# The last feed-forward net: chunk 3 by seven block products too, the half-wide chunk 5 by eight

## The chip, the cores and the metric

One core of one Trainium2 chip runs the whole program. The metric is the device time of one execution in microseconds, the median of the runs. The engines are named as the profile names them: PE (TensorE), DVE (VectorE), ACT (ScalarE), POOL (GpSimd) and SP (SyncE), which issues most DMAs.

## The reference

Two layers, each with a gated feed-forward net, a mixer (short convolution, a gated recurrence, pooled windows), cross attention against a memory of 256 rows, and a second feed-forward net; a layer norm stands behind each. There are 256 tokens of width 1024, all in float32. What matters here is the net:

```python
def swiglu(x, w_gate, w_up, w_down):
    return (jax.nn.silu(x @ w_gate) * (x @ w_up)) @ w_down
...
    h = layer_norm(ALPHA * h + 0.5 * swiglu(h, ffn2_gate[l], ffn2_up[l], ffn2_down[l]),
                   ln_g[l, 3], ln_b[l, 3])
```

`w_gate` and `w_up` are 1024 x 2816, `w_down` is 2816 x 1024. The change touches only the last of the four nets (`ffn2` of the second layer); its output is the kernel's output.

## The kernel before

**Products in three parts.** Each float32 operand is split into a rounded high part (ACT, a cast, L75) and the rest (DVE, a subtraction, L76). A product is then three matmuls: high by high, high by low, low by high (`mm_rows`). Weights come from HBM in pieces of 128 x 1024 floats (512 KB) into tiles called `raw` (six buffers); the two parts of a piece go to `whi` and `wlo` (eight buffers each), which come free when PE has used them.

**Chunks.** The hidden width 2816 is cut into five chunks of 512 and one of 256 (chunk 5). For each chunk a net computes gate and up products, the gated activation in the tile `sg`, turns it by four DMAs (`dealt`, L525) and a transpose on DVE (L531, into the buffer with the tag "up"), splits it into `ah` and `al`, and later multiplies it with the rows of `w_down` in slabs of 256 rows: `both(c, u)` is slab u of chunk c, 24 matmuls of 512 columns, which add to four PSUM banks `ys` (`dn` in the profile). Tokens come in two tiles of 128.

**Three ways to do a chunk.**
- `hidden` (by eight): gate, then up, each 2 token tiles x 8 k tiles x 3 matmuls of 512 columns, 96 in all.
- `by_seven`: with tokens and k halved, the four blocks of gate and up (first and second k half: `w00` gate first, `w10` gate second, `w01` up first, `w11` up second) need seven products of blocks rather than eight, each 4 k tiles x 3 matmuls. For this the weight blocks are added in place: `parts_of(r, plus)` adds one block to another on DVE (L702) and splits the sum, and `more` adds the second k half's block onto `w01` and then onto `w00` by accumulating DMAs from POOL's queue (L738). The sums of the token blocks (`bx`, in `kTh` and `kTl`) are made once per net. Two products stay in the tile `ef` (tag "up", one buffer) until the end of the chunk. Between the block products it runs two slabs of earlier chunks (`between`). For chunk 5 the matmuls have 256 columns.
- `last_hidden` (half-wide, in columns): four calls of `mm_cols`, each 8 matmuls of 512 columns and 8 of 256. Its result comes out turned already, so that no `dealt` DMAs are needed. Until now only the first net uses it.

**Homes of the blocks.** In `by_seven` the list `homes` says in which tiles the blocks `w00`, `w01`, `w11` and `w10` lie: pairs of one-buffer tiles ("spare0", "spare1"), ("lng", "lnb"), two `raw` buffers, and for `w10` "spare2" and one `raw`.

**Which chunk goes which way.** `sevens` is (2, 4) in the first net and (2, 4, 5) in the others. `later` says how many slabs run behind a chunk that is not by seven. Because chunk 5 by seven follows chunk 4 by seven, its turn is put off, and the last down products (`ending`) begin with token tile 0 over both column halves.

**The turned memory.** `mT` holds the transposed attention memory in two tiles with the tags "mT0" and "mT1", 2048 floats per partition each. Its last reader is the value product of the last attention.

**What sets the order.** The program is traced as written above; a planner then orders each engine's queue by its own estimate of when operands and buffers are ready, earlier traced work first, and each engine works its queue strictly in that order. `issue_after` puts an instruction behind another on its engine.

Of the kernel before, what the change touches and what calls it, by code (L numbers as in the profile page):

```python
# [8 lines left out]
F32 = mybir.dt.float32  # L9
# [8 lines left out]
P = 128  # L18
DEPTH = 2
SEQ = 256  # L20
DM = 1024
# [39 lines left out]
def model(ctx: ExitStack, tc: tile.TileContext, t: dict, out: bass.AP):  # L61
    nc = tc.nc
    cst = ctx.enter_context(tc.tile_pool(name="cst", bufs=1))
# [126 lines left out]
    mT = Halves()  # L190
# [285 lines left out]
    def ffn(l, name, n, pend=None, last=False, early=None, started=None, following=None):  # L476
        gate, up, down = (t[f"{name}_{x}"][l] for x in ("gate", "up", "down"))
        with tc.tile_pool(name="ffn", bufs=2, reuse_waits="tile") as fp:
            acts = []
# [10 lines left out]
            def all_products(w):  # L490
                o = [acc((P, CHUNK)) for _ in range(NT)]
                for a in range(0, NK, 2):
                    for i in range(NT):
                        for k in range(a, a + 2):
                            products(o[i], w, i, k)
                return o

            def activations():
                return fp.tile([P, NT, CHUNK], F32, tag="sg", name="sg", bufs=1)
# [9 lines left out]
            def activate(s, i, og):  # L509
                return nc.scalar.activation(ordered(s[:, i, :]), in_order(og), AF.Silu)  # L510

            def gated(s, i, ou):
                v = ordered(s[:, i, :])
                nc.vector.tensor_tensor(v, in_order(ou), v, op=ALU.mult)
# [120 lines left out]
            def hidden(c0, between=lambda: None):  # L635
                s = activations()
                o = all_products(load(gate, 0, NK, c0, CHUNK))
                for i in range(NT):
                    activate(s, i, o[i])
                between()  # L640
                o = all_products(load(up, 0, NK, c0, CHUNK))
                for i in range(NT):
                    gated(s, i, o[i])
                return turn(s)
# [17 lines left out]
                    split(*parts[n], q[o])  # L662
                return parts

            def by_seven(c0, ncol, bx, between):
                deep = 1024 // ncol

                def rows_by_columns(r):
                    return r.rearrange("p (k c) -> p k c", c=ncol)

                def pieces(*tags):
                    return [
                        rows_by_columns(
                            (fp if "spare" in g else wp).tile([P, DM], F32, tag=g, name="raw", bufs=6 if g == "raw" else 1)
                        )
                        for g in tags
                    ]

                def part_of(m, j, i):
                    k = 4 * j + deep * i  # L680
                    return m[k * P : (k + deep) * P, c0 : c0 + ncol].rearrange("(k p) c -> p k c", p=P)

                def block(m, j, to):
                    for i, x in enumerate(to):
                        loads.append(nc.sync.dma_start(x, part_of(m, j, i)))
                    return to

                if ncol == CHUNK:
                    homes = [("spare0", "spare1"), ("lng", "lnb"), ("raw", "raw")]
                    n = sevens.index(c0 // CHUNK)  # L690
                    homes = [homes[(n + i) % 3] for i in range(3)] + [("spare2", "raw")]
                else:
                    homes = [("spare2",), ("raw",), ("raw",), ("raw",)]
                w00 = block(gate, 0, pieces(*homes[0]))
                w01 = block(up, 0, pieces(*homes[1]))
                w10 = block(gate, 1, pieces(*homes[3]))

                def parts_of(r, plus=None):
                    hi, lo = [], []
# [15 lines left out]
                def run(o, x, w, more=False):  # L715
                    for k in range(4):
                        wh, wl = w.at(k, slice(0, ncol))
                        mm_rows(o, x[0][:, k, :], x[1][:, k, :], wh, wl, k == 0 and not more, k == 3, more)
# [27 lines left out]
                run(o, part_of_x(0, 1), parts_of(w10), True)  # L746
                between[0]()
                activate(s, 0, o)
                w11 = block(up, 1, pieces(*homes[2]))
                run(total, bx[1], parts_of(w00, w11), True)  # L750
                if ncol == CHUNK:
                    more(w00, gate, 1)
# [29 lines left out]
            def last_hidden(c0, turn=None):  # L782

                ah, al = act_tiles()
                s = activations()[:, 0, :].rearrange("p (j c) -> p j c", j=2)
                r = fp.tile([P, NT, CHUNK], F32, tag="up", name="up", bufs=1)[:, 0, :].rearrange("p (j c) -> p j c", j=2)
                for m, o in ((gate, s), (up, r)):
                    if turn and m is gate:
                        with tc.issue_after(passed[-1][1].ins):
                            turn(0, 0)  # L790
                    w = load(m, 0, NK, c0, 2 * P)
                    if turn and m is gate:
                        with tc.issue_after(lows[-1].ins):
                            turn(0, 2)
                    for j in range(2):
                        add(o[:, j, :], mm_cols(w, slice(j * P, (j + 1) * P), xT))
                    if m is gate:
                        nc.scalar.activation(s, s, AF.Silu)
                nc.vector.tensor_tensor(s, r, s, op=ALU.mult)
                for j in range(2):  # L800
                    split(
                        *(x[:, j, :].rearrange("p (i b r) -> p i b r", i=2, b=4) for x in (ah, al)),
                        s[:, j, :].rearrange("p (i r b) -> p i b r", i=2, b=4),
                    )
                if turn:
                    with tc.issue_after(lows[-1].ins):
                        turn(1, 0)
                        turn(1, 2)
                return ah, al
# [4 lines left out]
                return w, ah[:, 2 * u : 2 * u + 2, :], al[:, 2 * u : 2 * u + 2, :]  # L814


            sevens = (2, 4) if early is not None else (2, 4, 5)
            passed, dealts, turn_memory = [], [], None
            bx = []

# [6 lines left out]
            chunks = [(c, min(CHUNK, DFF - c)) for c in range(0, DFF, CHUNK)]  # L827
# [13 lines left out]
                            rows_of(a, i, k, m, c == u == k == 0, apart)  # L841

            todo = [(c, u) for c in range(4) for u in range(2)]
            later = (0, 0, 0, 2, 0, 2) if early is None else (0, 1, 0, 1, 0, 2)
            for c, (c0, ncol) in enumerate(chunks):
                if not c:
                    acts.append(first()())
                    ys = [[acc((P, 512), "dn") for _ in range(2)] for _ in range(NT)]
                elif c in sevens:
                    half = []  # L850

                    def deal_last():
                        acts[4] = acts[4]()

                    left = by_seven(
                        c0, ncol, bx,
                        [lambda: both(*todo.pop(0))] * 2 if ncol == CHUNK else
                        [lambda: (half.append(slab(3, 0)), both(3, 0, half[0], (0,))), deal_last, lambda: both(3, 0, half[0], (1,))],
                    )
                else:  # L860
                    acts.append(hidden(c0)() if ncol == CHUNK else last_hidden(c0, turn_memory))
                if c == 1 and early is None:
                    bx.extend(blocks_of_x())
                if c == 5:
                    gb = ln_params(l, n)
                if c == 1 and early is not None:

                    with tc.issue_after(loads[-1].ins):
                        rest = early(fp)
                if c == 3 and early is not None:  # L870
                    with tc.issue_after(lows[-1].ins):
                        rest[0]()
                    nc.gpsimd.tensor_copy(early_memory[:, 0:2048:256], acts[2][0][:, 0, 0:8].bitcast(F32))
                    turn_memory = load_memory(fp, loads[-1])
                if c in sevens:
                    if ncol < CHUNK:
                        held = []
                        with tc.issue_after(lows[-1].ins):
                            acts[4] = acts[4](held)
                    acts.append(left() if c + 1 in sevens else left()() if c == 5 else left()()())  # L880
                    if ncol < CHUNK:
                        with tc.issue_after(passed[-1][0].ins), tc.issue_after(passed[-1][1].ins):
                            held[0]()
                        both(3, 1)
                else:
                    for _ in range(later[c]):
                        both(*todo.pop(0))
# [569 lines left out]
```

## Time and profile before

| | |
|---|---|
| runs | median 1063.42 us (1062.63 to 1063.47, 3 runs) |
| profiled execution | 1062.76 us; span 1061.1 us; granted clock 0.998 |
| PE busy | 99% of the span, 6014 matmuls |
| DVE, ACT, POOL busy | 87%, 62%, 9% |
| DMA | 251.06 MB, mean 237 GB/s |
| last net | about 887 to 1061 us |

Times in rows of the profile are microseconds from the start of the span. A row of a timeline has start, duration, engine, line and operation, the tiles written and read, a count where equal instructions were merged, and in brackets the time that the engine stood idle before it and what ended that. In a table of stretches each engine has its busy time and, in brackets, its instructions; then come the granted clock of PE, the busy share of the 16 DMA engines and GB/s.

### The profile page before, as it was taken

The page shows a single profiled execution, that of the slowest core. Times are in us where ns is not written, and L with a number is a line of the kernel's source. Part 1 is how long each engine was busy: PE and PEld are TensorE (multiplying, and loading weights), DVE is VectorE, ACT ScalarE, POOL GpSimd, SP SyncE. Part 2 cuts the span into 40 slices and gives each one's busy share as a digit, 9 for nine tenths or more (in the row PEclk, how much of TensorE's full clock was granted, in tenths as well). Part 3 has the DMA queues.
Part 4 walks back from the last instruction along what each step waited for, and adds up shares of the span by engine and source line. Part 5 has one row for each costly group of instructions (what it writes and reads, how often), then busy time and mean ns, then how long its engine had stood idle before and what let it go on. Part 6 is the DMA issues. An engine that isn't in the chain of part 4 may idle for free.

```text
span 1061.1 us, 16463 instructions
## 1 busy us (share of the span) xinstructions
PE 1051.1 (99%) x6014; PEld 934.2 (88%) x6014; DVE 922.6 (87%) x1224; ACT 662.1 (62%) x909; POOL 94.6 (9%) x128
## 2 busy tenths in 40 slices
PE   9999999999999999999999999999999999999997
PEld 7888888889899888888888888998998998888896
DVE  6998898989988789887898887999899788898787
ACT  6675775676557567655665656666774655675661
POOL 8002001000000001010001001010000000000001
PEclk9999999999999999999999999999999999999999
DMA  9999984754675589988689978876636675799961
GB/s 363 296 301 298 260 274 156 256 167 156 211 273 178 167 281 232 349 200 224 237 302 257 335 226 210 268 233 223 207 117 219 241 240 167 241 295 301 242 194 68
DMA packets 142305, 251.06 MB, mean 237 GB/s; under 512 B 11248, under 2 KB 51984, under 8 KB 142224
## 3 DMA queue, kind: packets, MB, share of 16 engines
q1 hardware_dynamic: 130656, 228.89, 64.9%
q0 software_dynamic: 10992, 19.94, 11.0%
q10 hardware_dynamic: 576, 1.18, 0.3%
q8 instruction: 47, 0.77, 0.3%
q14 instruction: 34, 0.28, 0.1%
HBM read 234.50 MB, written 1.05 MB: 222 GB/s over the span
## 4 chain that ended last, share of the span: by engine, by line
PE 99%; DMA 1%; DVE 0%; issue 0%; ACTq 0%; DVEq 0%
PE acc L132 65%; PE dn L132 31%; PE acc L199 1%; DMA h<-in_x_dram 1%; PE dn L1135 0%; PE dn L1209 0%; PE dn L1208 0%; PE dn L1197 0%; PE acc L1277 0%; PE dn L1160 0%; DVE h L412 0%; PE acc L581 0%; PE acc L338 0%; DVE h L407 0%; DVE st L383 0%
## 5 line engine op out<-in xcount | busy, mean ns | idle before, releaser
L76 DVE TENSOR_TENSOR wlo<-raw,whi 128x1024 fp32r<-128x1024 f32 (+1 forms) x452 | 533.1, 1209 | 60.7 <-ACT whi L75 54.5
L75 ACT CAST whi<-raw 128x1024 fp32r<-128x1024 f32 (+1 forms) x452 | 456.2, 1043 | 196.5 <-PE dn L132 58.3
L132 PE MATMUL acc<-whi,xT 128*128 128x512 f32 (+1 forms) x1064 | 313.8, 372 | 0.0
L132 PEld LDWEIGHTS acc<-whi,xT 128*128 128x128 f32 x1064 | 199.1, 189 | 27.2 <-DVE halves L721 0.4
L132 PE MATMUL acc<-wlo,xT 128*128 128x512 f32 (+1 forms) x532 | 197.9, 372 | 0.0
L132 PE MATMUL dn<-whi,ah 128*128 128x512 f32 x346 | 131.5, 380 | 0.0
L132 PE MATMUL dn<-wlo,ah 128*128 128x512 f32 x346 | 131.2, 379 | 0.0
L132 PE MATMUL dn<-whi,al 128*128 128x512 f32 x346 | 131.1, 379 | 0.0
L132 PE MATMUL acc<-xT,whi 128*128 128x512 f32 x480 | 117.6, 381 | 0.0
L132 PEld LDWEIGHTS acc<-wlo,xT 128*128 128x128 f32 x532 | 100.6, 189 | 13.2
L132 PEld LDWEIGHTS acc<-xT,whi 128*128 128x128 f32 x480 | 86.8, 190 | 9.8
L132 PE MATMUL dn<-whi,xT 128*128 128x512 f32 x288 | 87.8, 381 | 0.0
L132 PEld LDWEIGHTS dn<-whi,al 128*128 128x128 f32 x346 | 65.4, 189 | 9.2
L132 PEld LDWEIGHTS dn<-wlo,ah 128*128 128x128 f32 x346 | 65.4, 189 | 8.9
L132 PEld LDWEIGHTS dn<-whi,ah 128*128 128x128 f32 x346 | 65.4, 189 | 8.9
L132 PEld LDWEIGHTS acc<-xT,wlo 128*128 128x128 f32 x480 | 62.9, 191 | 3.2
L132 PE MATMUL acc<-xT,wlo 128*128 128x256 f32 x480 | 63.3, 275 | 0.0
L132 PE MATMUL acc<-whi,kTh 128*128 128x512 f32 (+1 forms) x176 | 62.0, 352 | 0.0
L132 PE MATMUL acc<-wlo,kTh 128*128 128x512 f32 (+1 forms) x176 | 61.7, 351 | 0.0
L132 PE MATMUL acc<-whi,kTl 128*128 128x512 f32 (+1 forms) x176 | 61.7, 351 | 0.0
L132 PEld LDWEIGHTS dn<-whi,xT 128*128 128x128 f32 x288 | 54.4, 189 | 7.7 <-DVE xT L76 0.2
L132 PE MATMUL dn<-wlo,xT 128*128 128x512 f32 x144 | 54.6, 379 | 0.0
(250 smaller groups left out, 1279.9 us busy)
## 6 DMA issues: line engine op xcount, KB each, us to landing
raw<-in_ffn_up_dram SPq DMA_DIRECT2D x88, 512.0 KB, 6.0
raw<-in_ffn_down_dram SPq DMA_DIRECT2D x88, 512.0 KB, 6.0
raw<-in_ffn_gate_dram SPq DMA_DIRECT2D x84, 512.0 KB, 5.8
raw<-in_w_in_dram SPq DMA_DIRECT2D x48, 512.0 KB, 4.7
dealt<-sg SPq DMA_DIRECT2D x80, 128.0 KB, 4.9
raw<-in_ffn_up_dram POOLq DMA_DIRECT2D x19, 512.0 KB, 6.2
raw<-in_ffn_gate_dram POOLq DMA_DIRECT2D x16, 512.0 KB, 9.9
raw<-in_ca_k_dram SPq DMA_DIRECT2D x16, 512.0 KB, 5.4
```

Of the source, the lines that this page charges most:

```text
L75: rounded = nc.scalar.copy(hi, src)
L76: lows.append(nc.vector.tensor_tensor(lo, src, hi.bitcast(F32), op=ALU.subtract))
L132: turns.append(nc.tensor.matmul(o, w, x, start=start, stop=stop, skip_group_check=more))
L199: turns.append(nc.tensor.transpose(pt[:, k, :], src[:, (4 * j + k) * P : (4 * j + k + 1) * P], unit))
```

## The change

In the last net `sevens` becomes (2, 3, 4): chunk 3 is computed by seven block products, and chunk 5 goes through `last_hidden`. `later` becomes (0, 0, 0, 0, 0, 2): the two slabs that ran behind chunk 3 run inside it, and the two slabs of chunk 3 run behind chunk 5. The part of `by_seven` that lays out and loads the first two blocks becomes a function of its own, `blocks_of_weights`. For chunk 3 of the last net it is called right behind chunk 0 (`begun`), with `w00` and `w01` in the two tiles of the turned memory; `w11` lies in ("lng", "lnb"). Chunk 4 has `w00` in the spares, `w01` in two `raw` buffers and `w11` in "mT0". The other nets are as before.

```diff
-            def by_seven(c0, ncol, bx, between):
+            def blocks_of_weights(c0, ncol):
                 deep = 1024 // ncol
...
                 def pieces(*tags):
+                    if "mT" in tags[0]:
+                        x = cst.tile([P, 2 * DM], F32, tag=tags[0], name="raw")
+                        return [rows_by_columns(x[:, n * DM : (n + 1) * DM]) for n in range(2)]
                     return [
...
                     homes = [homes[(n + i) % 3] for i in range(3)] + [("spare2", "raw")]
+                    if last:
+                        homes[0:3] = (
+                            (("spare0", "spare1"), ("lng", "lnb"), ("raw", "raw")),
+                            (("mT0",), ("mT1",), ("lng", "lnb")),
+                            (("spare0", "spare1"), ("raw", "raw"), ("mT0",)),
+                        )[n]
                 else:
                     homes = [("spare2",), ("raw",), ("raw",), ("raw",)]
-                w00 = block(gate, 0, pieces(*homes[0]))
-                w01 = block(up, 0, pieces(*homes[1]))
-                w10 = block(gate, 1, pieces(*homes[3]))
+                w00, w01 = (block(m, 0, pieces(*x)) for m, x in zip((gate, up), homes))
+
+                def others(m, n):
+                    return block(m, 1, pieces(*homes[n]))
+
+                return w00, w01, others, part_of
+
+            def by_seven(c0, ncol, bx, between):
+                deep = 1024 // ncol
+                w00, w01, others, part_of = begun.get(c0) or blocks_of_weights(c0, ncol)
+                w10 = others(gate, 3)
...
-                w11 = block(up, 1, pieces(*homes[2]))
+                w11 = others(up, 2)
...
-            sevens = (2, 4) if early is not None else (2, 4, 5)
+            sevens = (2, 4) if early is not None else (2, 3, 4) if last else (2, 4, 5)
+            begun = {}
...
-            later = (0, 0, 0, 2, 0, 2) if early is None else (0, 1, 0, 1, 0, 2)
+            later = (0, 1, 0, 1, 0, 2) if early is not None else (0, 0, 0, 0, 0, 2) if last else (0, 0, 0, 2, 0, 2)
...
+                if c == 0 and last:
+                    begun[chunks[3][0]] = blocks_of_weights(*chunks[3])
...
-                    acts.append(left() if c + 1 in sevens else left()() if c == 5 else left()()())
+                    acts.append(left() if c == 4 and 5 in sevens else left()() if c == 5 else left()()())
```

More of the change, by code (lines that the diff above doesn't have):

```diff
@@ L691, in by_seven, with rows_by_columns @@
                     homes = [homes[(n + i) % 3] for i in range(3)] + [("spare2", "raw")]
+                    if last:
[4 more added lines that the diff above has]
+                        )[n]
                 else:
                     homes = [("spare2",), ("raw",), ("raw",), ("raw",)]
-                w00 = block(gate, 0, pieces(*homes[0]))
-                w01 = block(up, 0, pieces(*homes[1]))
-                w10 = block(gate, 1, pieces(*homes[3]))
+                w00, w01 = (block(m, 0, pieces(*x)) for m, x in zip((gate, up), homes))
[6 more added lines that the diff above has]
+                w10 = others(gate, 3)
+                def rows_by_columns(r):
+                    return r.rearrange("p (k c) -> p k c", c=ncol)
                 def parts_of(r, plus=None):
```

## The prediction

> **What bounds the kernel now.** I read the page's engine line first, then the chain that ended last, then the table by stretches of the last net, then the timelines of PE, DVE, ACT, POOL and SP around it. The page:
>
> ```profile
> span 1061.1 us, 16463 instructions
> PE 1051.1 (99%) x6014; PEld 934.2 (88%) x6014; DVE 922.6 (87%) x1224; ACT 662.1 (62%) x909; POOL 94.6 (9%) x128
> q1 hardware_dynamic: 130656, 228.89, 64.9%
> q0 software_dynamic: 10992, 19.94, 11.0%
> PE 99%; DMA 1%; DVE 0%; issue 0%; ACTq 0%; DVEq 0%
> ```
>
> The reader is to see that TensorE alone carries the time, and VectorE is second with 87%. The chain in order of time, at the end of the last net, gives the prices of a matmul where nothing waits:
>
> ```profile
> 1031.13 1.34 PE acc L132 x12
> 1032.47 16.84 PE dn L132 x78
> 1049.31 4.03 PE acc L132 x36
> 1053.36 0.43 DVE h L371
> 1057.11 0.40 DVE h L412
> ```
>
> 78 matmuls of 512 columns in 16.84 us are 0.216 us each; 12 of 256 columns in 1.34 us and 36 in 4.03 us are 0.112 us each. Inside the last net (887 to 1053 us) PE issues at these spacings throughout; the view of waits has no row for PE there. So work taken off PE comes off the time, and any new wait on PE is added to it. The four stretches below, cut where PE begins each chunk, are chunk 2 (by seven), chunk 3 (by eight), chunk 4 (by seven), and chunk 5 (by seven, half-wide) with what follows it; columns are busy time and instructions of PE, weight load, DVE, ACT, POOL, then granted clock, DMA share, GB/s.
>
> ```profile
> 929.50:958.00 28.50, 28.50 (x133) 24.90 (x133) 26.01 (x26) 20.31 (x24) 2.37 (x2) 1.00 1.04 314
> 958.00:989.10 31.10, 31.10 (x145) 27.23 (x145) 26.21 (x26) 15.74 (x18) 2.37 (x2) 1.00 0.94 272
> 989.10:1017.60 28.50, 28.50 (x133) 24.95 (x132) 22.63 (x21) 19.13 (x22) 3.69 (x3) 1.00 0.79 211
> 1017.60:1037.00 19.40, 19.40 (x131) 17.96 (x130) 17.45 (x19) 13.74 (x18) 1.44 (x2) 1.00 0.77 231
> ```
>
> PE fills every stretch at clock 1.00; DVE and the DMA engines are near full in 929 to 989, and that is where the change puts more on both.
>
> **PE work removed and added.** Chunk 3 goes from eight block products to seven: 8 x 12 = 96 matmuls of 512 columns become 84, so 12 x 0.216 = 2.6 us go. The 48 matmuls of its two down slabs stay. Chunk 5 goes the other way. By seven it was 84 matmuls of 256 columns, 84 x 0.112 = 9.4 us. In columns by eight it is four calls of `mm_cols` with 8 matmuls of 512 and 8 of 256 columns each. That form stands in the timeline of the query product (PE rows):
>
> ```profile
> 826.00 1.89 PE L132 MATMUL acc<-xT,whi 128*128 128x512 f32 x8
> 827.73 1.05 PE L132 MATMUL acc<-xT,wlo 128*128 128x256 f32 x8
> 828.62 1.89 PE L132 MATMUL acc<-xT,whi 128*128 128x512 f32 x8
> ```
>
> From 826.00 to 828.62 is one call, 2.62 us; four are 10.5 us, 1.1 us more than before. PE work falls by 2.6 - 1.1 = 1.5 us. The order of the last down products changes (token tile 0 is no longer run early over both halves), but not their number, and the last 36 matmuls and the 7.8 us from 1053.34 us to the end of the span (norm of the second tile, store) stay; I cost that at nothing, since the rows at 1053.36 and after hang on the last matmul, not on DVE's backlog. The DVE and ACT work that chunk 5 loses (three of seven pieces, three adds, a turn through four DMAs) lies beside PE; it is worth nothing in time.
>
> **The early loads.** Chunk 3's gate and up blocks of the first k half (four DMAs of 512 KB on SP) go into the two tiles of the turned memory, traced behind chunk 0. The memory's last reader is the value product of the attention before; its last row on PE, the SP timeline from there, and the DMA share behind it:
>
> ```profile
> 862.75 0.38 PE L132 MATMUL acc<-whi,mT 128*128 128x512 f32 x1
> ```
>
> ```profile
> 864.13 6.96 SPq L103 DMA_DIRECT2D raw<-in_ffn_up_dram  x4
> 871.19 0.41 SPq L685 DMA_DIRECT2D raw<-in_ffn_gate_dram  x1
> 885.71 0.37 SPq L103 DMA_DIRECT2D raw<-in_ffn_gate_dram  x1
> ```
>
> ```profile
> 872.00:880.00 8.00, 8.00 (x39) 7.01 (x38) 2.25 (x7) 0.60 (x2) 0.00 (x0) 1.00 0.48 178
> 880.00:887.00 7.00, 7.00 (x38) 6.20 (x37) 5.94 (x10) 4.65 (x7) 0.63 (x1) 1.00 0.09 9
> ```
>
> SP issues nothing between 871.6 and 885.7 because the six raw buffers are full, and the DMA engines stand at 0.48 and 0.09. By the page the hardware queue needs 0.649 x 1061.1 / 228.89 = 3.0 us of all engines per MB, so the 2 MB take 6 us out of some 10 free ones. Cost nothing. If they came later, chunk 1's loads would be pushed back by up to those 6 us; that is the bound above.
>
> **DMA in chunks 3 and 4.** A chunk by seven loads four 1 MB blocks plainly, adds two more with accumulating transfers issued from POOL, and reads two 1 MB down slabs. The software queue (mostly these) takes 0.110 x 1061.1 / 19.94 = 5.9 us per MB. Chunk 3 so gains 2 x 5.9 = 11.7 us of DMA and has 6 us moved ahead; chunk 5 drops 0.5 MB of accumulation, 2.9 us. The stretches 958 to 1017.6 held 0.94 x 31.1 + 0.79 x 28.5 = 52 us; they get 52 + 11.7 - 6 - 2.9 = 55 us in 57. Full, but not over.
>
> The transfer with the least room is the second accumulation of a chunk: piece split (DVE), POOL issues, landing, cast (ACT), split (DVE), PE. In chunk 2 the POOL timeline has it, each row with the landing that the trace gives for that line:
>
> ```profile
> 935.23 1.18 POOL L738 DMA_DIRECT2D raw<-in_ffn_gate_dram  x1 [8.06 <-DVE wlo L76]
> 938.75 1.19 POOL L738 DMA_DIRECT2D raw<-in_ffn_gate_dram  x1 [2.34 <-DVE wlo L76]
> ```
>
> ```profile
> DMA to landing us min/median/max: 10.2/10.2/10.2
> ```
>
> Landing is 10.2 us behind the second issue. PE uses the result in the last 12 matmuls of chunk 2, from 958.0 - 2.6 = 955.4 us, 6.5 us after that landing. In chunk 4 both landed within 10.6 us of their issues at 994.1 and 995.2:
>
> ```profile
> L738 POOL DMA_DIRECT2D raw<-in_ffn_gate_dram x2: 1180/1226/1272, 994.1 to 995.2; - x2
> ...
> DMA to landing us min/median/max: 6.0/8.3/10.6
> ```
>  By the sum below, chunk 3's second accumulation goes out at about 971; it lands at 981, cast and split end at 983.5, and PE wants that second piece at 985.3. Room of 1.8 us: no stall, though a thin margin.
>
> **VectorE, the term that decides.** Rows of DVE at the seam of chunks 2 and 3:
>
> ```profile
> 950.05 4.63 DVE L76 TENSOR_TENSOR wlo<-raw,whi 128x1024 fp32r<-128x1024 f32 x4 [1.33 <-ACT whi L75]
> 954.60 0.68 DVE L721 TENSOR_TENSOR halves<-halves,acc 128x512 f32<-128x512 f32 x1
> 955.19 2.35 DVE L76 TENSOR_TENSOR wlo<-raw,whi 128x1024 fp32r<-128x1024 f32 x2
> 960.33 1.22 DVE L775 TENSOR_TENSOR sg<-sg,halves 128x1024 f32<-128x1024 f32 x1
> 968.55 1.30 DVE L531 STREAM_TRANSPOSE square<-dealt 128x512 f32<-128x512 f32 x2 [0.18 <-DVE wlo L76]
> 971.60 1.23 DVE L76 TENSOR_TENSOR al<-square,ah 128x1024 fp32r<-128x1024 f32 x1 [0.63 <-ACT ah L75]
> ```
>
> One operation of 1024 columns costs DVE 1.14 us in a row of them (the fourth starts 3.41 us behind the first, at 1.22 us each). A chunk by seven has 18 splits (seven blocks and two slabs of two pieces), 4 adds (L702, the same shape), the gate product and the split behind the turn: 24 x 1.14 = 27.4 us, and 2 x 0.6 for L721 and 1.2 for L531: 29.8 us, against 28.5 us of PE (132 x 0.216). Chunk 3 by eight needs 12 splits, one turn and little else, some 17 us against 31. So today chunk 3 is where DVE catches up; after the change three chunks follow each other that each cost DVE 1.3 us more than PE, and only its lead carries it: at most eight pieces, the depth of `whi` and `wlo`.
>
> The lead at the seam: of the four splits from 950.05, two end chunk 2 (952.4) and two are chunk 3's first block (954.7). Then two L721 and the second block (two adds, two splits) end at 954.7 + 1.2 + 4.6 = 960.5; PE, starting chunk 3 at 958.0, wants that last piece three half-runs later, at 961.9. Lead 1.4 us. One chunk later DVE has 29.8 us behind it and PE 28.5, and the gate product of chunk 3 (1.14 us) now falls ahead of the same piece: 1.4 - 1.3 - 1.1 = -1.0. So a stall of 1.0 us in chunk 4, or none if the planner lets the gate product wait, which it can (its reader is a chunk away). Less than none is excluded, since PE has no wait to lose. The end above is a DVE that also waits: in 929.5 to 958 it was idle 28.5 - 26.0 = 2.5 us. If each of chunks 3 and 4 kept that, 1.0 + 5.0 = 6.0 us. I take 0.5, between the two placements, since the wait at 950.05 was for a cast that itself had waited for a landing, which a late DVE meets less.
>
> **What ACT waits for.** The copy out of chunk 3's second product goes into the one "up" buffer, which is free only when chunk 2's turned block is split (today 971.60 plus 1.2, 15 us into chunk 3). It stands in ACT's queue with casts behind it. The silu of chunk 3 likewise waits for the one `sg` buffer until chunk 2's four deal DMAs have landed (about 968.5). PSUM is not short: four banks, three in use at that time. If the planner knows these times, casts go ahead of the copy; today's nearest case is the silu at chunk 1, which held ACT:
>
> ```profile
> 918.59 0.60 ACT L510 ACTIVATE sg<-acc 128x512 f32<-128x512 f32 x1 [4.20 <-DMA dealt<-sg]
> ```
>
> ACT stood 4.2 us there and PE lost nothing, with eight pieces of lead. I cost it at nothing; the end above is again those 4.2 us, where DVE's lead is gone.
>
> **The sum.** -2.6 + 1.1 + 0.5 = -1.0 us. The profiled execution took 1062.76 us (span 1061.1 and 1.7 around it) and lies 0.66 under the median; from it 1061.8, from the median 1063.42 it gives 1062.4 us, which I forecast.
>
> **The rivals.** (a) VectorE becomes the bound, slower: its 2.5 us of waits come back in chunks 3 and 4, stall 6.0, -1.5 + 6.0 = +4.5 us, 1067.9. For it: 29.8 against 28.5 us, three times. Against: 1.4 us of room at the first seam, and the order is planned for both. It decides for slower once the stalls exceed 3.6 us. Chance 0.11. (b) The accumulating transfers land late, in full DMA engines: the 1.8 us of room in chunk 3 is spent, and each of chunks 3 and 4 waits 2 to 3 us: -1.5 + 5 = +3.5, 1066.9. For it: share 1.04 in chunk 2, 55 of 57 us. Against: the landings of chunk 4, of which PE made no stall. Chance 0.10. (c) No stall at all, the full 1.5 us: 1061.9; chance 0.30, on the same side of the bound as my forecast. (d) More than PE's arithmetic, 2.2 us or more, would need a gain at the tail, where the last rows hang on PE: chance 0.07, mostly scatter of the runs (1062.63 to 1063.47). (e) The early loads come too late to be early and chunk 1 waits up to 6 us: 1067.9; against it stand 14 us without an issue: 0.02. (f) An operation of DVE costs its whole 1.22 us also in a row of them: a chunk then has 24 x 1.22 + 2.4 = 31.7 us, the stall by the end of chunk 4 is 1.0 + 48 x 0.08 = 4.8 us, and the time -1.5 + 4.8 = +3.3, 1066.7. Against: four took 4.63 us, not 4.88. Chance 0.02. The Trainium skill ("VectorE: DVE Perf Modes", The DRAIN you can't avoid) has this as a rule: the next operation does not start until the pipe is empty. The trace of this case disagrees, by the 4.63 us. My case, stalls of 0.2 to 3.5 us: 0.38.
>
> **How the numbers follow.** 0.2% is 2.1 us, about what a measurement of this kernel can tell from no change. Within it lie (c) and mine, 0.68; slower are (a), (b), (e), (f), 0.25; faster (d), 0.07. The range runs from 1061.5 (no stall and some scatter) to 1066.5 (half the way of the stalls of (a), most of (b)); outside are the far part of (a) and (e), and part of (d).
>
> **What would show it.** Right: PE without a wait through chunk 3, 84 + 48 matmuls in 28.5 us; four more plain loads on SP between 864 and 885; chunk 5 in 10.5 us; DVE dense from 950 to 1010. Wrong: PE waits for `wlo` (DVE) in chunk 4's second or fourth product, for a cast behind a POOL transfer at a chunk's last product, or ACT standing on `halves` while PE waits. A gain over 2.1 us, or a loss with DVE idle and DMA idle, would break the account.

## The result and the profile after

The changed kernel takes 1069.28 us (median of 6 runs, 1067.31 to 1070.89) against 1063.14 us (1062.49 to 1064.06) of the kernel before beside it: ratio 1.0056, interval 1.0043 to 1.0069. It is slower by 6 us; 1062.4 was forecast, no change. Its profiled execution, one of 1068.87 us, has a span of 1067.2 us, 6.1 more than before. One execution below, of the kernel whose loads were traced later, took 3962.51 us and is left out of its median. From the page of the changed kernel:

```profile
span 1067.2 us, 16411 instructions
PE 1051.0 (98%) x5982; PEld 932.7 (87%) x5982; DVE 928.9 (87%) x1230; ACT 666.7 (62%) x916; POOL 97.0 (9%) x129
PE 86%; DVE 5%; issue 5%; DMA 3%; ACT 1%; POOL 0%; SPq 0%; DVEq 0%; POOLq 0%; ACTq 0%
```

PE has 32 fewer matmul records, VectorE 6 more instructions, and the chain of work that ended last, 99% PE before, now leaves it for VectorE, ACT and DMA. The view of PE's waits in the last net (885 to 1060 us), which had no row before, has two (total, times, longest), and the PE timeline has the five places:

```profile
PE acc L132 <- DVE halves L742: 4.4, 3, 1.9
PE dn L132 <- ACT whi L75: 2.5, 2, 1.3
```

```profile
957.66 0.48 PE L132 MATMUL acc<-whi,xT 128*128 128x512 f32 x1 [1.94 <-DVE halves L742]
964.38 1.13 PE L132 MATMUL dn<-whi,ah 128*128 128x512 f32 x4 [1.27 <-ACT whi L75]
989.28 0.46 PE L132 MATMUL acc<-whi,xT 128*128 128x512 f32 x1 [1.32 <-DVE halves L742]
995.91 0.92 PE L132 MATMUL dn<-whi,ah 128*128 128x512 f32 x3 [1.22 <-ACT whi L75]
1020.58 0.45 PE L132 MATMUL acc<-whi,xT 128*128 128x512 f32 x1 [1.09 <-DVE halves L742]
```

Measured from one start to the next less 0.216 us, they cost 2.10, 1.44, 1.48, 1.37 and 1.25 us: 7.6 together. Three stand ahead of the last product of chunks 2, 3 and 4, two ahead of the first matmuls of a down slab in chunks 3 and 4. From the start of its first matmul to that of its last, the net takes 172.31 us, where it took 165.81: 6.5 more. That is these 7.6, another 0.5 in the matmuls right behind each wait (the next starts 0.29 to 0.32 us later, not 0.216), and 1.6 less of work. Behind the last matmul's start 7.5 us follow, where 8.0 did, and so the spans differ by 6.1.

The chain of the changed kernel at the first of these places, in order of time:

```profile
939.81 11.32 DMA raw<-in_ffn_gate_dram
951.16 1.07 ACT whi L75
952.25 2.37 DVE wlo L76 x2
954.64 1.23 DVE raw L723
955.87 1.14 DVE wlo L76
957.00 0.60 DVE halves L742
```

An accumulating transfer issued at 939.81 lands 11.3 us later. The cast and the split of the piece that it brought follow; VectorE stood idle for 2.47 us until then. Behind them come a split, an addition and a split for chunk 3's first products, and only then L742, which is f = e - total (from VectorE's timeline):

```profile
952.25 2.36 DVE L76 TENSOR_TENSOR wlo<-raw,whi 128x1024 fp32r<-128x1024 f32 x2 [2.47 <-ACT whi L75]
...
956.92 0.68 DVE L742 TENSOR_TENSOR halves<-halves,acc 128x512 f32<-128x512 f32 x1
```

PE's last product writes the bank `total`, which L742 reads; it starts at 957.66, 0.06 us behind the end of L742. In the prediction's rows L721 (the same line) starts at 954.60 and takes 0.68, so `total` was free at 955.28. Before the change PE began there at:

```profile
955.45 0.38 PE L132 MATMUL acc<-whi,xT 128*128 128x512 f32 x1
```

The kernel before made it with 0.17 us to spare.

The accumulating transfer accounts for about half of this first wait. Counted from the net's first matmul (887.24 before, 887.34 after), it lands 2.09 us later: it takes 1.13 us longer (11.32 against 10.19), and it is issued 0.96 us later, because VectorE comes that much later to the splits ahead of it. VectorE was late from chunk 1's turn on, where the four `dealt` DMAs, issued at the same time, landed some 1 us later (before, then after):

```profile
918.61 1.30 DVE L531 STREAM_TRANSPOSE square<-dealt 128x512 f32<-128x512 f32 x2 [2.01 <-DMA dealt<-sg]
919.67 1.30 DVE L531 STREAM_TRANSPOSE square<-dealt 128x512 f32<-128x512 f32 x2 [3.06 <-DMA dealt<-sg]
```

The other kind of gap, in the ACT timeline of the changed kernel:

```profile
955.96 1.04 ACT L75 CAST whi<-raw 128x1024 fp32r<-128x1024 f32 x1 [1.86 <-DVE raw L723]
959.96 2.94 ACT L75 CAST whi<-raw 128x1024 fp32r<-128x1024 f32 x3 [2.96 <-DVE raw L723]
963.29 1.98 ACT L75 CAST whi<-raw 128x1024 fp32r<-128x1024 f32 x2
```

ACT takes its casts in order. It stands 1.86 and 2.96 us for additions (L723) on a VectorE that is late, and the slab's cast, behind them in the queue, goes out at 963.29; it takes 1 us, and PE was free for it at 962.94 (964.38 less the gap).

The table by stretches, columns as before:

```profile
872.00:880.00 8.00, 8.00 (x39) 7.00 (x38) 2.44 (x8) 0.50 (x2) 0.00 (x0) 1.00 1.00 364
929.50:958.00 28.50, 26.56 (x124) 22.94 (x123) 24.84 (x25) 17.88 (x21) 3.54 (x3) 1.00 1.03 292
958.00:986.50 28.50, 27.23 (x127) 23.52 (x125) 25.64 (x25) 19.42 (x23) 3.56 (x3) 1.00 0.96 241
986.50:1015.00 28.50, 25.96 (x119) 22.14 (x118) 28.11 (x27) 18.63 (x22) 4.83 (x4) 1.00 0.90 218
```

VectorE needs 29.8 us per chunk by the prediction's count, and 30.0 by this trace (busy time from the start of chunk 3's f at 988.45 to that of chunk 4's at 1019.76). In these stretches it is busy for 24.84, 25.64 and 28.11: idle 6.9 of 85.5 us. The row at 872 has the early loads, DMA at 1.00 where it stood at 0.48, and PE full.

### The profile page after: what moved, and what is told of

The parts are those of the page before. It is cut to its first block, busy times and chain, and to the rows that moved or that the text cites. A ratio compares the mean times of both kernels' runs of the same rounds, so it can differ in the third digit from the quotient of the medians.

```text
span 1067.2 us, 16411 instructions
## 1 busy us (share of the span) xinstructions
PE 1051.0 (98%) x5982; PEld 932.7 (87%) x5982; DVE 928.9 (87%) x1230; ACT 666.7 (62%) x916; POOL 97.0 (9%) x129
## 4 chain that ended last, share of the span: by engine, by line
PE 86%; DVE 5%; issue 5%; DMA 3%; ACT 1%; POOL 0%; SPq 0%; DVEq 0%; POOLq 0%; ACTq 0%
PE acc L132 56%; PE dn L132 27%; DVE wlo L76 3%; DMA raw<-in_ffn_gate_dram 2%; PE acc L199 1%; DMA dealt<-sg 1%; DVE raw L723 1%; PE dn L1159 0%; ACT whi L75 0%; POOL raw L759 0%; DMA h<-in_x_dram 0%; PE dn L1233 0%; DVE h L412 0%; PE acc L581 0%; DVE sg L514 0%
## 5 line engine op out<-in xcount | busy, mean ns | idle before, releaser
L132 PE MATMUL acc<-whi,xT 128*128 128x512 f32 (+1 forms) x1000 | 297.9, 375 | 4.4 <-DVE halves L742 4.4
L132 PEld LDWEIGHTS acc<-whi,xT 128*128 128x128 f32 x1000 | 187.7, 189 | 31.0 <-DVE halves L742 2.3
L132 PE MATMUL acc<-wlo,xT 128*128 128x512 f32 (+1 forms) x500 | 187.0, 374 | 0.0
L132 PE MATMUL acc<-xT,whi 128*128 128x512 f32 x512 | 125.3, 381 | 0.0
L132 PEld LDWEIGHTS acc<-wlo,xT 128*128 128x128 f32 x500 | 94.6, 189 | 12.6
L132 PEld LDWEIGHTS acc<-xT,whi 128*128 128x128 f32 x512 | 92.6, 190 | 10.5
L132 PEld LDWEIGHTS acc<-xT,wlo 128*128 128x128 f32 x512 | 67.1, 191 | 3.4
L132 PE MATMUL acc<-xT,wlo 128*128 128x256 f32 x512 | 67.5, 275 | 0.0
```

Of the source, the lines that this page charges most:

```text
L132: turns.append(nc.tensor.matmul(o, w, x, start=start, stop=stop, skip_group_check=more))
```

## The experiments

The theory had two parts. The last products wait for f, which stands behind splits that wait for a late accumulating landing (the *queue of f*). The slabs' casts wait behind additions on a VectorE that has too much work (the *slab casts*). Rivals: VectorE's work alone is too much, whatever the landings; or the early loads, or chunk 5, cost something.

**f from another bank.** `put(f, e, ALU.subtract, one if last else total)`.

> The changed kernel, but in the last net's chunks by seven the difference f is taken from the bank of the second product, not from the bank that the last product adds to; so PE's last product no longer waits for DVE's subtraction. The value of f is another. Theory A (PE waits for that one subtraction, which stands in DVE's queue behind splits that a late accumulating transfer holds up): the three gaps ahead of the last products of chunks 2, 3, 4 (2.1, 1.5, 1.3 us) vanish, the two at the first slab pieces (1.4 and 1.4) stay, about 1064.5 us. Theory B (DVE has too much work in chunks 2 to 4, whatever waits for it): the waits come back at other places, 1067 or more.

Measured 1066.0 us (1064.53 to 1069.85), ratio 1.0031 [1.0019, 1.0043], between the two expectations. PE's waits in the last net, in an execution of 1064.84 us:

```profile
PE dn L132 <- ACT whi L75: 3.7, 2, 2.0
```

The three waits for `halves` are gone, so the queue of f is what held those products; the slab waits grew from 2.5 to 3.7 us.

**No accumulation.** The transfers of the last net bring plain blocks: `accum_op=ALU.add` dropped there.

> The changed kernel, but in the last net the second k half's blocks are loaded over the first ones by plain transfers from the same queue, not accumulated; the sums are left out. Theory A in the form that the accumulating transfers land too late (10 to 11 us in chunks 2 to 4): landings of 5 to 7 us, DVE's splits behind them earlier by some 4 us, the gaps ahead of the last products gone, 1064 to 1065 us. Theory B: within 1 us of 1069, as DVE's work is the same.

Measured 1063.19 us, ratio 1.0001 [0.9991, 1.0010].

```profile
PE dn L132 <- ACT whi L75: 1.7, 2, 1.0
```

Chunk 2's two `gate` transfers land 7.7 and 6.2 us behind their issues, not 10.8 and 11.3 (this kernel, then the changed one):

```profile
DMA to landing us min/median/max: 6.2/7.0/7.7
DMA to landing us min/median/max: 10.8/11.1/11.3
```

VectorE does the same work in the same order, and in 85.5 us it is idle 2.8 us, not 6.9:

```profile
929.50:1015.00 85.50, 83.73 (x386) 72.37 (x385) 82.74 (x80) 61.51 (x72) 7.23 (x10) 1.00 0.81 265
```

So 6 us hang on the accumulation; what is left with VectorE's work alone is the 1.7 us at the slabs. The run does not separate the landings of these transfers from the load that they put on the DMA engines, whose share in these 85.5 us fell from 0.96 to 0.81.

**Additions of 64 columns.** VectorE's L723 does 64 of 512 columns in the last net, about 4 us less per chunk.

> The changed kernel, but in the last net the additions of weight blocks on DVE cover only 64 of 512 columns; every wait stays, and DVE loses about 12 x 0.9 = 11 us of work over chunks 2 to 4. The other columns' sums are left out. Theory B (DVE has too much work): all five gaps go, about 1062. Theory A (landing of the accumulating transfers, with the order of DVE's queue): the gaps ahead of the last products keep 1 us or more each, 1065 or more.

Measured 1067.09 us (1065.81 to 1068.62), ratio 1.0038 [1.0023, 1.0053].

```profile
PE acc L132 <- DVE halves L743: 2.5, 1, 2.5
```

The slab gaps are gone, and one wait for f is left, in chunk 3 behind a landing of 13.1 us; f now stands behind two additions and four splits there, as the planner had ordered that queue anew. Neither relief alone brings the predicted gain.

**Both.** No accumulation and additions of 64 columns.

> The changed kernel with both reliefs in the last net: the second k half's blocks loaded plainly over the first ones, and DVE's additions over 64 of 512 columns (both sums left out). Each relief alone took away one kind of gap. If the two kinds are all, PE has no wait left and the time is that of its matmuls: 1063.2 - 1.5 = 1061.7 us. If a third cause is hidden behind them, 1063 or more.

Measured 1060.62 us (1060.22 to 1060.97), ratio 0.9968 [0.9955, 0.9981]. PE has no wait in the last net, which takes 164.19 us from the start of its first matmul to that of its last, 1.6 less than before the change: the prediction's -1.5. What the block products cost on PE was right, and the two parts of the theory together are the whole stall. The time fell by 3.4 us, more than the 1.5 that was expected: the traces place 1.6 in the net and 0.6 behind its last matmul, and the rest stays open.

**Chunk 5 alone.** By eight, the rest as before the change: `sevens = (2, 4)`, no early blocks.

> Only the second half of the change: chunk 5 of the last net in columns by eight, chunk 3 by eight as before, no early loads. By the matmuls PE has 1.1 us more: 1064.3 us. If the new order at the end (no turn by DMAs, tile 0 not ahead) gains or costs by itself, that stands beside: below 1064.0 a gain, above 1065 a cost.

Measured 1064.15 us (1062.95 to 1066.16), ratio 1.0005 [0.9996, 1.0014]. Chunk 5's four calls take 10.5 us, as predicted. One wait has appeared:

```profile
PE acc L132 <- DVE halves L742: 0.9, 1, 0.9
```

It is chunk 2's last product, with landings of 10.6 and 11.1 us instead of 9.7 and 10.2: the margin of 0.17 us, spent without any change in chunk 3. That the time came out at the expected 1064.3 is partly luck: the wait, 1.1 us from start to start, was not in the sum, and what follows the last matmul took 7.3 us, not 8.0.

**Loads traced later.** The two blocks are traced ahead of chunk 3 instead of behind chunk 0: `if c == 2 and last`.

> The changed kernel, with chunk 3's two blocks loaded into the same tiles, but traced right ahead of chunk 3 rather than behind chunk 0. If the planner's SP queue then brings them in chunk 2, into full DMA engines, the accumulating transfers of chunk 2 land later and the time rises by 1 us or more over the changed kernel's 1069.3. If it places them in the idle stretch anyway, no change.

Measured 1069.06 us (1066.99 to 1071.42), ratio 1.0045 [1.0031, 1.0060], with gaps of 1.44, 1.43, 2.61 and 0.96 us. The planner put the loads at the same place all the same, from 871.02 to 875.0 us in SyncE's timeline:

```profile
871.02 1.53 SPq L688 DMA_DIRECT2D raw<-in_ffn_gate_dram  x3
872.65 2.34 SPq L688 DMA_DIRECT2D raw<-in_ffn_up_dram  x2
```

So this is the expectation's second case, and the run says nothing on what a late load would cost. It serves as a second look at the changed kernel.

**The second slab in halves**, one half before f's product and one behind:

```
 run(total, bx[2], parts_of(w01), True)
 put(f, e, ALU.subtract, total)
+if last: between[2]()
...
```

> The changed kernel with the second slab of each chunk by seven of the last net cut in two: one half ahead of the product whose sum f is taken from, the other behind it, so that DVE has 5.2 us rather than 2.6 us for f before PE's last product. Same work and same result. Theory A: the gaps ahead of the last products go (4.8 us), the ones at the first slab pieces stay, 1064.5 us; it would still not beat the kernel before. Theory B: the waits move to splits, 1067 to 1069.

Measured 1067.68 us (1067.45 to 1069.47), ratio 1.0046 [1.0031, 1.0061].

```profile
PE acc L132 <- ACT acc L775: 3.5, 3, 2.0
PE dn L132 <- ACT whi L75: 2.1, 2, 1.8
```

The waits for f are gone, and waits of 3.5 us together for ACT's negated copy (`less`), which half a slab no longer covers, stand in their place. The time is the one that theory B gave, by another wait than it named.

**The first slab early**, between a chunk's first and second product:

```
 nc.scalar.copy(total, o)
+if last: between[0]()
 run(one, bx[0], parts_of(w00, w01))
...
```

> The changed kernel, with the first slab of each chunk by seven of the last net between the first and the second block product rather than behind the third: DVE has 5.2 us more for the second block's additions and splits. Same work, same result. If the gaps at the slabs (1.4 and 1.4 us) come from DVE's additions, they go, and the gaps ahead of the last products shrink by what DVE catches up: 1065 to 1067 us. If the landing of the accumulating transfers alone is to blame, 1067 to 1069.

Measured 1066.13 us (1063.99 to 1067.95), ratio 1.0020 [1.0010, 1.0030].

```profile
PE acc L132 <- DVE halves L742: 3.7, 2, 2.6
```

The slab gaps go; the waits for f stay, with the longest at 2.6 us.

**f first in the queue.** f stands ahead of the last product's splits, everything computed:

```
+taken_f = put(f, e, ALU.subtract, total)
 run(less, bx[3], parts_of(w11), True)
...
+with tc.issue_after(taken_f.ins): w = parts_of(w00)
...
+run(total, part_of_x(1, 1), w, True)
```

> In the last net the subtraction f = e - total is put ahead of the two splits of the last product in VectorE's queue; the arithmetic is the changed kernel's. Theory 1 (queue order): TensorE's three gaps ahead of the last products (2.1, 1.5 and 1.25 us in the changed kernel) come from f standing behind splits that wait for an accumulating landing, so they shrink to under 0.7 us together, since one split of 1.1 us behind f fits into the 2.6 us of the fourth product. The gaps ahead of the slabs (1.4 and 1.4 us) stay or grow to some 4 us together, as they did where f was taken from another bank: time 1065 to 1066.5. Theory 2 (the landing itself): the last product needs the landed piece anyhow, so the wait only changes its name, from the subtraction to a split or a cast, total gaps stay at 7 to 8 us and the time at 1068 to 1069.5.

Measured 1071.72 us (1070.61 to 1072.58), ratio 1.0073 [1.0059, 1.0087]: outside both expectations. VectorE in chunk 2, then PE in chunk 3:

```profile
954.64 0.69 DVE L742 TENSOR_TENSOR halves<-halves,acc 128x512 f32<-128x512 f32 x1 [5.20 <-PE acc L132]
```

```profile
962.74 0.48 PE L132 MATMUL acc<-whi,kTh 128*128 128x512 f32 x1 [0.43 <-ACT whi L75]
965.07 0.48 PE L132 MATMUL acc<-wlo,kTh 128*128 128x512 f32 x1 [1.85 <-DVE wlo L76]
```

The gaps ahead of the last products are gone, as theory 1 of that run said. But VectorE now stands idle for 5.20 us until PE has made the fifth product, whose sum f is taken from, with the splits behind it, and comes late to the next chunk's second product. I had priced the order and not the idle time that it gives an engine without any to spare.

**Both orders.** f first and the first slab early.

> The same order for f, and the first slab of each chunk between its first and second products instead of behind the third; nothing is left out. Theory 1 (two orders, each with its own gap): both kinds of gap fall, to 1 us together or less, no stretch at half clock, and the time is 1061 to 1063, up to 2 us under the kernel before. Theory 3 (VectorE and the transfers have too much work whatever the order): a gap closed in one place opens in another, 3 to 5 us stay, time 1065 to 1068.

Measured 1068.57 us (1068.44 to 1069.29), ratio 1.0046 [1.0033, 1.0058]. The gaps moved, as its theory 3 had it. The waits in PE's view come to 4.0 us, within the 3 to 5 that it gave; with the slower matmuls around them (a stretch at half the granted clock among them, see below) the net takes 172.72 us, 8.5 more than with both reliefs:

```profile
PE acc L132 <- ACT whi L75: 1.7, 2, 0.9
PE acc L132 <- DVE wlo L76: 1.6, 2, 0.8
PE dn L132 <- ACT whi L75: 0.7, 2, 0.5
```

**Additions on GpSimd.** The second piece's addition of each block: `adder = nc.gpsimd if last and ncol == CHUNK and i else nc.vector`.

> The changed kernel, with two of the four additions of each by-seven chunk of the last net (the second piece of each block) on GpSimd in place of VectorE; nothing is left out. Theory 1 (VectorE's own time is what is short: its work plus its waits for landings and for TensorE): VectorE has 2 x 1.14 = 2.3 us less per chunk, 27.5 us of work against TensorE's 28.5, so the slab gaps (2.8 us together) close as they did where all additions were narrowed, the gaps at the last products (4.8 us) stay: time 1064 to 1067.5. Rival (GpSimd is no help): an addition of 1024 columns has no row on GpSimd in these traces; its fill of 1024 columns takes 0.95 us and its operation of 4 columns 1.07 us. If the addition takes 4 us or more, or VectorE's operations grow beside it, TensorE waits for the second pieces at the second and fourth product too and the time is 1070 us or more.

Measured 1083.12 us (1082.08 to 1084.44), ratio 1.0188 [1.0174, 1.0202]. The group of these additions, and VectorE's timeline beside one of them, which ran from 958.58 to 961.23:

```profile
L724 POOL TENSOR_TENSOR raw<-raw 128x1024 f32<-128x1024 f32 x6 | 18.4, 3066 | 11.6 <-DVE wlo L76 11.6
```

```profile
957.27 1.22 DVE L76 TENSOR_TENSOR wlo<-raw,whi 128x1024 fp32r<-128x1024 f32 x1
959.00 3.31 DVE L76 TENSOR_TENSOR wlo<-raw,whi 128x1024 fp32r<-128x1024 f32 x1
966.37 3.40 DVE L797 TENSOR_TENSOR sg<-sg,halves 128x1024 f32<-128x1024 f32 x1
```

The rival's second half: an addition is 3.07 us on GpSimd, and the VectorE operation that meets one grows from 1.22 to 3.3 or 3.4 us. VectorE gives away 1.14 us and loses 2.1. The split that began at 959.00 ended at 962.31, 1.08 us behind the addition beside it: it seems to have stood until that ended. The operation of 966.37 ended 1.09 us behind another addition (965.40 to 968.68). The Trainium skill ("SBUF — State Buffer", SBUF: two separate sides) has the rule: VectorE and GpSimd share a pair of ports as a lock, and an operation of VectorE with two SBUF inputs and one of GpSimd that reads SBUF don't overlap; the later one blocks until the first is done. The two rows agree with it, and the expectation should have had it.

**The same, first slab early.**

> The same, with the first slab of each by-seven chunk between the first and the second product; nothing is left out. Theory 1: VectorE has work 1 us per chunk below TensorE's and more time ahead of the additions, so of the slab-first kernel's gaps (4.2 us and a stretch at half clock, 1066.1 us) those that come from a late VectorE go and only what the landings of 10 us cost stays: 1061 to 1064. Rival (GpSimd's addition is long or slows VectorE): above 1067.

Measured 1078.19 us (1076.75 to 1080.25), ratio 1.0139 [1.0126, 1.0153]; waits for f of 11.0 us in three places. No kernel here that computes the reference beats the one before.

VectorE's and PE's idle time in 929.5 to 1015 us, 85.5 less the busy sums of the table by stretches, for the kernels that give VectorE the same work, with the ratio to the kernel before beside each:

| kernel | VectorE idle, us | PE idle, us | ratio |
| --- | --- | --- | --- |
| no accumulation | 2.8 | 1.8 | 1.0001 |
| first slab early | 4.7 | 2.2 | 1.0020 |
| f from another bank | 5.4 | 3.7 | 1.0031 |
| changed kernel | 6.9 | 5.8 | 1.0056 |
| loads traced later | 8.3 | 5.0 | 1.0045 |
| halved slabs | 8.5 | 5.7 | 1.0046 |
| both orders | 9.2 | 4.3 | 1.0046 |
| f first | 10.6 | 7.1 | 1.0073 |

The ends of the table stand in the order of VectorE's idle time, the middle does not: from 6.9 to 9.2 us of it the ratio does not rise. VectorE also waits for PE, so the table shows that the two idle times grow together and not which comes first. That a wait of VectorE is not made good later in these three chunks is likely by it, and not shown.

## Why the prediction was wrong

**Right:** PE's work fell by 1.5 us (1.6 in the kernel with both reliefs), chunk 5 by eight took 10.5 us, VectorE's work was 30.0 us per chunk against the 29.8 counted, and the early loads, issued from 871.37 to 875.2 us, cost nothing: PE is full behind them and begins the net at 887.34, where it began at 887.24. The tail, also put at nothing, was 0.5 us shorter: 7.5 us behind the last matmul's start, 8.0 before.

**The failed term is the stall, put at 0.5 us and measured at 7.6.** It came out of two steps.

1. "VectorE, the term that decides" summed work (29.8 against 28.5 us) and lead, and took 0.5 between 0 and 6.0. The end of 6.0 was right in kind: VectorE's waits came back, 6.9 us in three chunks. The reason given against it, that a late VectorE meets less of a cast's wait, holds only if it is late when the landing comes. It was not: at 952.25 in chunk 2 it waited 2.47 us for the cast of the landing, where it had waited 1.33 before.

2. "Room of 1.8 us: no stall", and "PE uses the result 6.5 us after that landing", followed the landed piece to the matmuls that read it. They left out who else stood in VectorE's queue behind its splits: f, and through the bank `total` the same matmuls. Counted that way the room in chunk 2 was 0.17 us, readable from the prediction's own row at 954.60 and its 955.4 us for PE. Of the four splits from 950.05 it took two for chunk 2's, but by the landings (944.93 and 948.95) only the first can be; three were chunk 3's, and f stood behind all four. In chunk 3 the piece itself had room, as predicted: it landed at 983.94, and PE was free for it at 987.8. But f began only at 988.45, and PE waited. In the kernel with chunk 5 alone the landing came 1.2 us later against PE's turn, and that cost 1.08 us.

"What ACT waits for", costed at nothing, held the right place and the wrong partner. No copy or silu held ACT in a way that cost PE; additions on VectorE did, and the slab's casts stood behind them. The rows quoted there (4.2 us of ACT that cost nothing) came from a chunk with eight pieces of lead, as the text itself said.

**The rivals.** (a) had the stall (6.0 us, 1067.9) and (b) the trigger (late landings, 1066.9); at 0.11 and 0.10 I treated them as alternatives. The runs show them as one mechanism with two exits: a late landing leaves VectorE idle, and the time lost appears at f and at the slabs. Without the accumulation the whole 6 us go (ratio 1.0001 against 1.0056); with narrow additions alone, about 2 (1.0038). (c), no stall, is the kernel with both reliefs, and not this one. (e) fell: PE had no wait in chunk 1. For (f) no run was needed: VectorE's splits still start 1.14 us apart. The section of the Trainium skill that the prediction names at (f) goes on to say that an operation that is not held starts earlier than the rule has it, so these rows do not contradict it as the prediction says.

**Open:** why the landings of chunk 2 went from 10.2 to 11.3 us and those of chunk 1's `dealt` DMAs by about 1 us, when neither chunk's transfers changed. The first moved to 11.1 with chunk 5 alone too, and the DMA share of that stretch was 1.04 before and 1.03 after. Over all the kernels here VectorE's wait for `dealt` in chunk 1 lies between 0.87 and 3.06 us, so part of it may be scatter from one execution to the next; each kernel has one trace.

## What to carry to other kernels

When a change fills the second busiest engine, count its waits as work: with the same work for VectorE and the same order, PE's waits came to 6.9 us in the changed kernel and to 1.7 us without the accumulation. To find the room behind a transfer, don't stop at the instruction that reads it; list what is queued behind that reader, and which buffers or banks those instructions free for the bound engine. An order that closes one gap must be priced by the idle time that it gives the full engine elsewhere.

## What the runs showed of the hardware

**In these traces the granted clock halves behind pauses of PE from about 2 us on.** In the kernel with narrow additions PE waited 2.50 us up to 987.33; the stretches with that wait and behind it:

```profile
984.00:988.00 4.00, 1.50 (x7) 0.99 (x7) 3.97 (x6) 3.41 (x4) 2.38 (x2) 1.00 1.01 307
988.00:991.00 3.00, 3.00 (x9) 2.40 (x8) 3.00 (x4) 1.62 (x2) 0.00 (x0) 0.52 1.12 203
```

The granted clock is 0.52 for some 3.4 us, and matmuls start 0.43 us apart instead of 0.216, which costs about 1.7 us on top of the wait. Waits of 2.03 us (GpSimd and first slab early), 2.04 (halved slabs), 2.45 (loads traced later) and 2.64 (first slab early) were followed by the same; 1.94 (the changed kernel) and 2.02 (f from another bank) were not. The rows of 2.03 and 2.02:

```profile
957.43 0.48 PE L132 MATMUL acc<-whi,xT 128*128 128x512 f32 x1 [2.03 <-DVE halves L743]
```

```profile
962.63 1.13 PE L132 MATMUL dn<-whi,ah 128*128 128x512 f32 x4 [2.02 <-ACT whi L75]
```

The Trainium skill ("TensorE: Matmul & The Clock Gate", HAM oscillation) states the danger for pauses of more than about 3.4 us; these traces have it from 2.03 us on, so these loops had less room than the page gives. With both orders 0.53 (1009.0 to 1011.2 us) came behind three gaps of 0.7 to 1.04 us within 4.5 us, so a row of short pauses can do it as well. The changed kernel's first wait, 1.94 us, lies just below; that its runs spread over 3.6 us, where the kernel before spread over 1.6, goes with it (mean granted clock 0.999 in the run of 1067.31 us, 0.997 in that of 1070.89), though only its profiled execution shows where.

**Accumulating transfers** of 512 KB landed 5.6 to 13.1 us behind their issue in the last net of the kernels without additions on GpSimd; plain transfers in their place took 3.8 to 8.3 us. In the changed kernel the one issued at 956.17 took 5.8 us and the one at 939.81 took 11.3, with the DMA share at 0.94 (956 to 966 us) and 1.07 (939 to 951).
